# Scheduling a 2387-us hybrid trunk kernel with the detailed machine model instead of the plain one

## The chip, the cores and the metric

The kernel runs on one NeuronCore of a Trainium2 chip. The metric is the device time of one execution in microseconds, taken as the median over runs. Each engine of the core (TensorE for matmuls, VectorE, ScalarE, GpSimd, and SyncE, which here only issues DMAs) works through its own list of instructions in the order in which the compiler left it, and waits at an instruction until the semaphores it needs have been raised by the others. In the rows below PE is TensorE, DVE is VectorE, ACT is ScalarE, SP is SyncE.

## The reference

Input is x of shape (1, 512, 1024) in float32. Each of two layers computes

```
h = RMSNorm(x)
P = h @ W_in            # columns for four mixers and four gates
A: Mamba-2 SSD          # chunked scan, 8 chunks of 64 rows
B: DSA sparse attention # 8 heads, 4 query tiles of 128 rows
C: RWKV-7               # delta-rule state, 8 heads, 8 chunks of 64 rows
D: S5                   # diagonal complex SSM
m = sum_n sigmoid(gate_n(h)) * (y_n @ W_branch_n);  x = x + m @ W_out
x = x + SwiGLU(RMSNorm(x))
```

and a final RMSNorm follows. All of it is float32.

## The kernel before

The large products (projections, gates, branch products, W_out and the feed-forward) are the **bulk**. A weight panel of 128x1024 is loaded into one of two `raw` buffers by a DMA on SP's queue (L286), cast to `wh` on ScalarE (L287), and the remainder `wl` is subtracted on VectorE (L288). For each 128x512 result TensorE then does three matmuls for each of eight slices of the depth: `hh` by `wh` (L294), `hl` by `wh` (L295) and `hh` by `wl` (L296), 24 matmuls in all. What they write is named `pj` (projections and gates), `pb` (branches) or `pf` (feed-forward).

The **mixers** are chains of small steps.

- `dsa()` (L601-666) has 32 steps: 8 heads, each with four query tiles of 128 rows against 128, 256, 384 and 512 keys. A step is a product `lgp` (L645), a bias add (L647), a masked maximum (L648), its negation (L651), an exponential on ScalarE (L652), a reciprocal (L653), a scaling (L654), transposes `ptp` (L657), a copy (L659) and the product with the values, `po` (L661).
- `rwkv_half()` (L1085-1304) runs twice, for heads 0-3 (half 0) and 4-7 (half 1). It forms the blocks of a triangular system (`rwA` L1157, masked on VectorE L1159, scaled L1161), sends them to DRAM (L1168) and back into another layout `NZ` (L1173), copies (L1175) and inverts them in 30 steps of two VectorE instructions (L1180, L1182), sends the inverse to DRAM (L1183, L1185) and back (L1188, L1190), completes it with small products (`zx` L1195, `zz` L1200), and then scans the eight chunks one after another: `bkt` (L1212, L1216), `rwP` (L1233, L1236), a copy on ScalarE (L1240), `rwU` (L1243), an add on VectorE (L1245), `rwS` (L1252), the state's update on VectorE (L1257, L1259), and the output `rwP` (L1264). Each chunk needs the state of the last.
- `ssd()` (L1308-1460) and `s5()` (around L883-1015) are similar; S5 loads its input with eight DMAs per half (L971, `s5UX`).

`Trunk.layer(i)` traces all this in program order:

```python
        with self.at("m", "Tb"):
            self.s5("B")
        with self.at("m", "Ta"):
            y[1] = self.dsa("A")
        self.fill(FILL[0])
        ...
            self.rwkv_half(0, y[2], "B")
        self.fill(FILL[1])
        with self.at("m", "Ta"):
            self.rwkv_half(1, y[2], "A")
        self.fill(FILL[2])
        with self.at("m", "Tb"):
            y[0] = self.ssd("B")
```

`fill(n)` traces n gate panels of bulk, and `FILL = (22, 4, 6)` (L63) says how many stand after which mixer. `at(kind)` gives what is traced a priority: weight loads come before mixers, mixers before bulk. The tile context then plays the program on a model of the machine: at each point it appends to an engine's list that instruction which the model holds to be ready and whose priority is first. So the priorities and the model's durations together fix the order of each list, and on the chip that order is kept. PSUM has two buffers for bulk results and three for each of the two mixer tags, and half 1 of RWKV uses the working slots that DSA frees.

The whole is one launch:

## Time and profile before

| | before |
| --- | --- |
| three runs | 2386.46, 2387.46, 2395.36 us; median 2387.46 us |
| profiled execution, span from first to last instruction | 2387.2 us |
| TensorE busy | 2337.6 us, 98% |
| VectorE busy | 1448.5 us, 61% |
| ScalarE busy | 909.7 us, 38% |
| GpSimd busy | 103.5 us, 4% |
| mean granted TensorE clock | 0.988 of full speed |

The profiled execution's span lies 0.3 us under the median of the runs, so what lies around the span is left out of account, and a sum can be made against 2387.2 us. A matmul's shown time overlaps that of the next; the interval from start to start says what one costs TensorE when it doesn't wait.

### The profile page before, as it was taken

How to read it: one execution, taken by the hardware profiler on the slowest of the kernel's cores; microseconds unless marked ns; L12 is line 12 of the kernel's file. 1: busy time of each engine (PE TensorE's matmuls, PEld its weight loads, DVE VectorE, ACT ScalarE, POOL GpSimd, SP SyncE). 2: the span in 40 equal slices, each digit the busy share in tenths (PEclk: the TensorE clock that was granted, in tenths of full speed). 3: DMA queues.
4: the chain of work that ended last, by engine and by line, in shares of the span. 5: the costliest groups of instructions: out<-in, count | busy, mean ns of one | idle time of the engine just before them, and what ended most of it. 6: DMA issues, size and time to landing. Idle time of an engine off the chain costs nothing.

```text
span 2387.2 us, 32092 instructions
## 1 busy us (share of the span) xinstructions
PE 2337.6 (98%) x12348; PEld 1858.2 (78%) x12348; DVE 1448.5 (61%) x2744; ACT 909.7 (38%) x1459; POOL 103.5 (4%) x180
## 2 busy tenths in 40 slices
PE   7999999999999999999999999999999999999998
PEld 5887767777778888887878787677777788888786
DVE  6569656767578687543343693578667775444333
ACT  6342454434452343322232334543345433222222
POOL 3210000000000101000021000000000000000000
PEclk9999999999999999999998999999999999999999
DMA  7545442334157435433375454324242663333332
GB/s 213 131 114 153 120 157 80 100 94 133 41 175 228 117 100 161 127 97 102 114 198 129 119 158 132 118 83 110 67 142 65 205 194 91 97 97 97 92 97 84
DMA packets 421680, 294.18 MB, mean 123 GB/s; under 512 B 56624, under 2 KB 378240, under 8 KB 419928
## 3 DMA queue, kind: packets, MB, share of 16 engines
q1 hardware_dynamic: 412016, 265.58, 38.0%
q0 software_dynamic: 8512, 26.43, 4.1%
q8 instruction: 97, 1.59, 0.3%
q14 instruction: 55, 0.45, 0.1%
q10 hardware_dynamic: 1000, 0.13, 0.0%
HBM read 237.27 MB, written 51.40 MB: 121 GB/s over the span
## 4 chain that ended last, share of the span: by engine, by line
PE 89%; DVE 5%; DMA 1%; issue 1%; ACT 1%; SPq 0%; POOL 0%; DVEq 0%; ACTq 0%; POOLq 0%
PE pj L295 18%; PE pj L294 18%; PE pj L296 18%; PE pf L296 3%; PE pf L294 3%; PE pf L295 3%; PE pb L294 3%; PE pb L296 2%; PE pb L295 2%; PE lgp L645 2%; PE po L661 2%; DVE wl L288 1%; PE rwA L1157 1%; PE ptp L657 1%; PE rwP L1236 1%
## 5 line engine op out<-in xcount | busy, mean ns | idle before, releaser
L294 PE MATMUL pj<-hh,wh 128*128 128x512 f32 x1888 | 750.0, 398 | 2.8 <-ACT hh L274 1.5
L296 PE MATMUL pj<-hh,wl 128*128 128x512 f32 x1888 | 746.9, 396 | 1.0 <-DVE wl L288 1.0
L295 PE MATMUL pj<-hl,wh 128*128 128x512 f32 x1888 | 747.9, 396 | 0.0
L287 ACT CAST wh<-raw 128x1024 fp32r<-128x1024 f32 x336 | 348.8, 1038 | 947.2 <-PE pj L295 370.6
L288 DVE TENSOR_TENSOR wl<-raw,wh 128x1024 fp32r<-128x1024 f32 x336 | 405.0, 1205 | 388.4 <-ACT wh L287 379.4
L294 PEld LDWEIGHTS pj<-hh,wh 128*128 128x128 f32 x1888 | 355.5, 188 | 85.3 <-issue 7.6
L296 PEld LDWEIGHTS pj<-hh,wl 128*128 128x128 f32 x1888 | 355.1, 188 | 81.0 <-issue 5.8
L295 PEld LDWEIGHTS pj<-hl,wh 128*128 128x128 f32 x1888 | 355.3, 188 | 80.6 <-issue 6.9
L294 PE MATMUL pf<-hid,wh 128*128 128x512 f32 x352 | 137.9, 392 | 1.6 <-ACT wh L287 1.6
L296 PE MATMUL pf<-hid,wl 128*128 128x512 f32 x352 | 137.7, 392 | 0.5 <-DVE wl L288 0.5
L295 PE MATMUL pf<-hid,wh 128*128 128x512 f32 x352 | 137.0, 390 | 0.0
L294 PE MATMUL pb<-yh,wh 128*128 128x512 f32 x256 | 101.8, 398 | 0.0
L295 PE MATMUL pb<-yl,wh 128*128 128x512 f32 x256 | 100.7, 393 | 0.0
L296 PE MATMUL pb<-yh,wl 128*128 128x512 f32 x256 | 100.4, 392 | 0.0
L528 DVE TENSOR_TENSOR fa<-fa,pj 128x512 f32<-128x512 f32 x44 | 30.2, 686 | 95.4 <-PE pj L296 95.3
L525 DVE TENSOR_TENSOR fa<-pj,rb 128x512 f32<-128x512 f32 x44 | 30.4, 690 | 88.7 <-PE pj L296 88.7
L294 PEld LDWEIGHTS pf<-hid,wh 128*128 128x128 f32 x352 | 66.1, 188 | 16.8 <-ACT wh L287 3.4
L296 PEld LDWEIGHTS pf<-hid,wl 128*128 128x128 f32 x352 | 66.1, 188 | 16.0 <-DVE wl L288 2.6
L295 PEld LDWEIGHTS pf<-hid,wh 128*128 128x128 f32 x352 | 66.1, 188 | 13.5
L652 ACT ACTIVATE lg<-lg,nm 128x128 f32<-128x128 f32 (+1 forms) x64 | 35.9, 561 | 78.0 <-DVE nm L651 77.8
L294 PEld LDWEIGHTS pb<-yh,wh 128*128 128x128 f32 x256 | 48.1, 188 | 11.5 <-issue 0.8
L661 PEld LDWEIGHTS po<-p_t,qkvo 128*64 128x64 f32 x320 | 33.2, 136 | 29.8 <-ACT p_t L659 21.1
(482 smaller groups left out, 3144.5 us busy)
## 6 DMA issues: line engine op xcount, KB each, us to landing
raw<-in_w_in SPq DMA_DIRECT2D x146, 512.0 KB
raw<-in_ffn_w SPq DMA_DIRECT2D x120, 512.0 KB
gates<-gate SPq DMA_DIRECT2D x64, 256.0 KB
gld<-gates SPq DMA_DIRECT2D x64, 256.0 KB
raw<-in_w_branch SPq DMA_DIRECT2D x32, 512.0 KB
raw<-in_w_out SPq DMA_DIRECT2D x16, 512.0 KB
raw<-in_ffn_w SPq DMA_DIRECT2D x16, 384.0 KB
s5xs<-s5UX SPq DMA_DIRECT2D x16, 256.0 KB
```

Of the source, the lines that this page charges most:

```text
L287: nc.scalar.copy(wh[:, :n], raw[:, :n])
L288: nc.vector.tensor_sub(wl[:, :n], raw[:, :n], wh[:, :n].bitcast(F32))
L294: mm(ps, wh, ah, start=first, stop=False)
L295: mm(ps, wh, al, start=False, stop=False)
L296: mm(ps, wl, ah, start=False, stop=last)
L525: nc.vector.tensor_mul(a, p1, rb)
L528: nc.vector.tensor_mul(a, a, p3)
L645: mm(ps[:, :W], q[rows, qt * 128:(qt + 1) * 128], k[rows, :W], start=True, stop=True)
L652: nc.scalar.activation(t[:, :W], t[:, :W], AF.Exp, bias=nm, accum_out=sm[:, qt:qt + 1])
L657: nc.tensor.transpose(pt[:, b * 128:(b + 1) * 128], t[:, b * 128:(b + 1) * 128], self.ident)
L661: mm(po[rows, qt * 128:(qt + 1) * 128], vt[:, b, rows], p_t[:, b * 128:(b + 1) * 128], start=(b == 0), stop=(b == qt))
L1157: mm(pa[:, (c - c0) * 128:(c - c0 + 1) * 128], BK[rows, hp, c], AR[rows, hp, c], start=True, stop=True)
```

## The change

```diff
-    with tile.TileContext(nc) as tc:
+    with tile.TileContext(nc, schedule_with_timeline_sim=True) as tc:
         trunk(tc, ins, out)
```

The program, its buffers, priorities, shapes and counts stay. TensorE, VectorE, GpSimd and SP have the same instructions as before; ScalarE has 15 fewer loads of its function tables (37 where 52 were). What the change moves is the order on each engine, since the model that decides what is ready is another one. Bulk and mixer work alternate on TensorE 333 times before and 175 times now. Three places show it.

On TensorE, a chunk of the scan of RWKV half 0 in layer 0 (`rwP`, `rwU`, `rwS` with the matrix M; `pj` is bulk; `lgp`, `ptp`, `po` belong to attention). Before, from the fourth chunk:

```order
L1236 MATMUL rwP<-UV,M_3260 64x64 x2
L294 MATMUL pj<-hh,wh 128x512
L295 MATMUL pj<-hl,wh 128x512
L296 MATMUL pj<-hh,wl 128x512
L294 MATMUL pj<-hh,wh 128x512
L1243 MATMUL rwU<-rwPe,M_3259 64x64 x2
L1243 MATMUL rwU<-rwPe,M_3260 64x64 x2
L295 MATMUL pj<-hl,wh 128x512
L296 MATMUL pj<-hh,wl 128x512
L294 MATMUL pj<-hh,wh 128x512
L295 MATMUL pj<-hl,wh 128x512
L1252 MATMUL rwS<-UV,bkts 128x128 x2
```

And the same place of the fourth chunk in the changed kernel:

```order
L1236 MATMUL rwP<-UV,M_3260 64x64 x2
L657 MATMUL ptp<-cst,lg 128x128 x2
L645 MATMUL lgp<-qkvo 128x384
L1243 MATMUL rwU<-rwPe,M_3259 64x64 x2
L1243 MATMUL rwU<-rwPe,M_3260 64x64 x2
L661 MATMUL po<-p_t,qkvo 64x128 x2
L1252 MATMUL rwS<-UV,bkts 128x128 x2
L1264 MATMUL rwP<-UV,M_3259 64x64 x2
```

The bulk has gone from between the steps of the chunk and a step of attention stands there. Over the eight chunks of half 0 there stood 72 bulk matmuls (59 in layer 1) and now stands none; three heads of attention, which before had ended by then, take part of the room. The bulk that stood here went to earlier places: the early steps of attention now have 18 to 100 bulk matmuls between them. Between the last `rwA` of half 0 and its first `zx` stood 228 bulk matmuls in layer 0 and 207 in layer 1; now 87 and 85 stand there, with some 34 instructions of attention. For half 1 the numbers at that place are 190 and 203 before, and 231 in both layers now. In the scan of half 1, 57 and 55 bulk matmuls stood between first and last chunk; now 38 stand there, all near its first and last chunk, and the six chunks in the middle share TensorE with 111 small matmuls of SSD alone.

On VectorE, the start of the inversion of half 0 in layer 0 (L1175 copies what the load L1173 brought; L647 to L654 belong to attention). Before:

```order
L647 TENSOR_TENSOR lg<-lgp,bias 128x256
L648 ISA lg,mx<-lg,mask 128x256
L648 ISA mx 128x1
L1175 COPY NZ<-NZ 64x1024
L651 TENSOR_SCALAR nm<-mx 128x1
L1180 TENSOR_TENSOR rwv<-NZ 64x30
L1182 TENSOR_TENSOR NZ<-NZ,rwv 64x30
```

And in the changed kernel:

```order
L1159 TENSOR_TENSOR M_3260<-rwA,cst 128x512 x2
L1161 TENSOR_TENSOR M_3260<-M_3260,rwrn 64x16x64
L288 TENSOR_TENSOR wl<-raw,wh 128x1024
L1175 COPY NZ<-NZ 64x1024
L1180 TENSOR_TENSOR rwv<-NZ 64x30
L1182 TENSOR_TENSOR NZ<-NZ,rwv 64x30
L1180 TENSOR_TENSOR rwv<-NZ 64x58
L1182 TENSOR_TENSOR NZ<-NZ,rwv 64x29x2
```

The copy that waits for the way through DRAM and back now stands one instruction behind L1161, whose result is sent on that way; before, 18 rows of attention and `wl` stood between the two. In layer 0 half 1 and layer 1 half 1 it is also one instruction now (10 and 11 rows before), in layer 1 half 0 six (16 before).

On SP's queue, the loads of S5's input in layer 1. Before:

```order
L949 DMA ud<-us 128x512
L971 DMA s5UX<-ud 16x16x64
L286 DMA raw<-in_w_in 128x8x128
L971 DMA s5UX<-ud 16x16x64 x2
L286 DMA raw<-in_w_in 128x8x128
L971 DMA s5UX<-ud 16x16x64
L286 DMA raw<-in_w_in 128x8x128
L971 DMA s5UX<-ud 16x16x64
L286 DMA raw<-in_w_in 128x8x128
```

And in the changed kernel:

```order
L286 DMA raw<-in_w_in 128x8x128
L971 DMA s5UX<-ud 16x16x64 x6
L286 DMA raw<-in_w_in 128x8x128
L949 DMA ud<-us 128x512
L971 DMA s5UX<-ud 16x16x64 x2
L949 DMA ud<-us 128x512
L286 DMA raw<-in_w_in 128x8x128
L987 DMA s5xs<-s5UX 64x1024
```

The eight loads stood between weight loads, each of which waits for a free `raw` buffer; now they stand nearly together.

## Rows read from the trace of the kernel before

**Rows 1.** The page: engines' busy time, and the chain that ended last

```profile
PE 2337.6 (98%) x12348; PEld 1858.2 (78%) x12348; DVE 1448.5 (61%) x2744; ACT 909.7 (38%) x1459; POOL 103.5 (4%) x180
...
PE 89%; DVE 5%; DMA 1%; issue 1%; ACT 1%; SPq 0%; POOL 0%; DVEq 0%; ACTq 0%; POOLq 0%
```

**Rows 2.** Stretches: length, each engine's busy time, granted clock, DMA share, GB/s

```profile
720.00:780.00 60.00, 60.00 (x267) 49.68 (x266) 49.39 (x69) 16.93 (x21) 0.00 (x0) 1.00 0.69 222
...
1293.80:1310.80 17.00, 17.00 (x69) 15.94 (x69) 1.75 (x2) 1.17 (x2) 4.99 (x7) 0.50 0.39 118
1205.00:1211.80 6.80, 5.26 (x16) 3.77 (x16) 5.11 (x9) 2.41 (x4) 0.06 (x1) 0.50 0.64 224
```

**Rows 3.** What PE waited for: us in all, times, longest

```profile
PE xtp L213 <- DMA cst<-in_cst: 14.3, 1, 14.3
PE ptp L657 <- DVE lg L654: 4.7, 7, 1.2
PE s5py L1012 <- DVE s5xs L1005: 4.2, 3, 2.6
PE nrms L249 <- DVE acc L241: 2.9, 1, 2.9
...
PE zx L1195 <- DMA zts<-zt: 0.3, 1, 0.3
```

**Rows 4.** Timeline, DVE, inversion's start in half 0: start, duration, instruction

```profile
422.40 1.22 DVE L1161 TENSOR_TENSOR M<-M,rwrn 64x1024 f32<-64x1024 f32 x1
...
438.64 0.68 DVE L1175 COPY NZ<-NZ 64x1024 f32<-64x1024 f32 x1
```

**Rows 5.** Timeline of SP's queue, the load that this start waits for

```profile
433.35 0.46 SPq L1173 DMA_DIRECT2D NZ<-zd  x1
```

**Rows 6.** DVE's groups in the stretch of that inversion, 439 to 484

```profile
L1180 DVE TENSOR_TENSOR rwv<-NZ 64x30 f32<-64x30 f32 (+14 forms) x30 | 9.6, 321 | 0.5
L1182 DVE TENSOR_TENSOR NZ<-NZ,rwv 64x30 f32<-64x30 f32 (+14 forms) x30 | 9.5, 317 | 0.4
L288 DVE TENSOR_TENSOR wl<-raw,wh 128x1024 fp32r<-128x1024 f32 x6 | 7.3, 1215 | 0.9 <-ACT wh L287 0.9
```

**Rows 7.** Timeline of DVE, SP's queue and PE: the inversion's end to zx

```profile
483.38 0.17 DVE L1182 TENSOR_TENSOR NZ<-NZ,rwv 64x30 f32<-64x30 f32 x1
...
491.35 0.46 SPq L1188 DMA_DIRECT2D zts<-zt  x1
...
495.96 1.19 PE L1195 MATMUL zx<-zts,M 32*32 32x32 f32 x32
```

**Rows 8.** PE's groups between the last rwA and zx, 424 to 496

```profile
L294 PE MATMUL pj<-hh,wh 128*128 128x512 f32 x73 | 29.0, 398 | 0.0
```

**Rows 9.** Timeline of one chunk of the scan, half 0, layer 0

```profile
518.79 0.28 PE L1243 MATMUL rwU<-rwPe,M 64*64 64x64 f32 x2
...
519.10 0.42 DVE L1245 TENSOR_TENSOR UV<-rwU,rwrn 64x256 f32<-64x256 f32 x1 [3.26 <-PE rwU L1243]
...
523.99 0.26 ACT L1240 COPY rwPe<-rwP 64x128 f32<-64x128 f32 x1 [0.52 <-PE rwP L1236]
...
524.30 0.67 PE L1243 MATMUL rwU<-rwPe,M 64*64 64x64 f32 x8
```

**Rows 10.** PE's groups in that scan, 511 to 556

```profile
L296 PE MATMUL pj<-hh,wl 128*128 128x512 f32 x25 | 11.1, 442 | 0.0
```

**Rows 11.** Timeline of one step of attention at 512 keys, layer 0

```profile
396.22 1.12 PE L645 MATMUL lgp<-qkvo 64*128 64x512 f32 x2
...
397.27 0.87 PE L661 MATMUL po<-p_t,qkvo 128*64 128x128 f32 x6
...
398.07 0.50 PE L295 MATMUL pj<-hl,wh 128*128 128x512 f32 x1
...
401.40 0.60 PE L657 MATMUL ptp<-cst,lg 128*128 128x128 f32 x4
...
401.93 0.48 PE L645 MATMUL lgp<-qkvo 64*128 64x128 f32 x2
```

## The prediction

> **What bounds the kernel now.** I read the page first. TensorE is busy 98% of the span and carries 89% of the chain that ended last [rows 1]. The list of its waits confirms that: after the 14.3 us for the constants at the start there are fifteen further entries, from 4.7 us down to 0.3 [rows 3], 26 us together. Then the stretches: in one that holds only bulk, 267 matmuls take 60.00 us, so a bulk matmul costs 0.2247 us, and the clock is at its full level [rows 2]. So the time before is TensorE's own work. A new order can win little, since those 26 us are all that could be saved; it can lose whatever waits it brings. The question is where TensorE's list no longer holds enough independent work to cover the mixers' chains. I went through the new order with the durations of the old trace.
>
> **The change part by part.** The same places occur in both layers, so I price one layer and double it. Bulk moved out of a stretch costs the same where it goes; what counts is the cover that is missing.
>
> *Inversion of half 0.* Before, between the last product `rwA` and the first `zx`, 72 us pass, with 73 bulk matmuls of each of the three lines (219 recorded) beside attention [rows 8]. In the new order 87 (85) bulk matmuls stand there and 33 (36) instructions of attention: 87 × 0.2247 = 19.5 us and some 9.5 us, together 29 us of cover. Attention's 9.5 us come from its step at 512 keys: the products take 1.05 us (396.22 to 397.27), `po` 0.80 (397.27 to 398.07), the transposes 0.53 (401.40 to 401.93) [rows 11]; that is 2.4 us, about 1.5 for the mean over the four widths, and five to six steps stand there.
> The chain to be covered is: the product L1161, 1.2 us; the way through DRAM, from 423.62 (422.40 + 1.22) to the copy at 438.64, 15.0 us [rows 4]; the inversion's 60 instructions, 9.6 + 9.5 = 19.1 us [rows 6]; the way back, from 483.55 to `zx` at 495.96, 12.4 us [rows 7]. The two ways include time in queues. Their lower bounds: the load alone took 438.64 − 433.35 = 5.3 us [rows 4, 5], on the way back 495.96 − 491.35 = 4.6 us [rows 7]; a store and a load as long give 10.6 and 9.2. I take 13 and 12, between them. VectorE now stops at the copy while the DMA runs, because the copy stands directly behind L1161 and the engine works in order. So the `wl` subtractions for the 87 matmuls (four at 1.2 us, [rows 6]) and the VectorE part of attention (five steps of some 1.5 us) come behind the copy, into the inversion: I take 28 us for it, with 19 and 31 as bounds. Sum 1.2 + 13 + 28 + 12 = 54 us against 29: **25 us** of waiting (bounds 11 and 30). Before, the same chain cost nothing because 219 bulk matmuls lay over it.
>
> *Scan of half 0.* Here no bulk stands any more. A chunk's chain took 5.5 us from `rwU` (518.79) to the next `rwU` (524.30) [rows 9], some bulk included. In the stretch of the scan 25 matmuls of each bulk line (about 74) take 16.6 us of 45 [rows 10], so TensorE's own part is 28 us for seven and a half chunks, 3.7 us each. Three heads of attention, twelve steps of 1.5 us, now lie in the scan: 18 us. With `zx`, `zz` and the output's products the stretch holds about 57 us of TensorE work. The chain is 7 us for `zx` and `zz` (four rounds of 1.2 us and the copies between), eight chunks, and about 8 us of normalisation at the end, where before 32 bulk matmuls lay. A step of attention has its own chain from `lgp` to `ptp`, 396.22 to 401.40, 5.2 us [rows 11], which uses VectorE and ScalarE too, and both chains wait for each other on each in-order list. I take 7 us a chunk instead of 5.5: 7 + 56 + 8 = 71, less 57: **14 us** (bounds 0, if a chunk stays at 5.5, and 26, at 8.5).
>
> *Inversion of half 1.* Now 231 bulk matmuls, 52 us, against 1.2 + 13 + 19 + 12 us and ten `wl` in between (12 us): 57. The `wl` that stand behind the copy are late as well while VectorE waits 13 us, and the panels that TensorE has ready run out. **8 us** (0 to 15).
>
> *Scan of half 1.* The six middle chunks have 111 small SSD matmuls beside them and no bulk. TensorE's work there is about 31 us, 5.2 per chunk; at 7 us per chunk **11 us** are missing (0 to 20, the latter since SSD's own chain uses VectorE and ScalarE).
>
> Warm, that is 25 + 14 + 8 + 11 = 58 us a layer (11 to 91).
>
> *The clock.* [...] If all of the scan of half 0 ran at 0.50, a chunk with its attention would need 2 × (3.7 + 1.7) = 10.8 us instead of 7, 30 us over eight chunks, and with the ends 38; the six chunks of half 1 2 × 5.2 = 10.4 instead of 7, 20, with the ends 25. That is 63 us a layer at most and 0 at least; I take half, **32 us**.
> [...]
>
> *S5 at the start of layer 1.* Its input loads stand together on SP now, so S5 can begin sooner, and the 17.0 us stretch at half clock behind its wait may vanish: **−8 us** (0 to −15, with the waits for `s5xs` and the norm, 4.2 and 2.9 us, partly saved [rows 3]). The 15 ScalarE table loads that vanish lie under TensorE's work; without that cover, inside the chains, they would give back a microsecond or two of the waits above. I count them at nothing.
>
> Sum: 2 × (58 + 32) − 8 = 172 us. On 2387.2 us that is **2559, rounded 2560 us**; the median of the runs is 0.3 us higher than the span, which changes nothing.
>
> **The rivals.**
> *The clock stays low through both scans.* Then 63 instead of 32 a layer: 2387 + 2 × 121 − 8 = 2621 us. [...] With every bound at its worst, 2 × (91 + 63) gives 2695.
> *Only the waits count.* The clock recovers between them: 2387 + 116 − 8 = 2495; with the waits at half their size 2440.
> *The cover suffices.* If the round trips go at their bounds, and attention's steps and the chunks dovetail as the model that ordered them assumes, nothing is lost: 2387 ± 12 us, the change doesn't move the time. For it: the scheduler chose these places as ready. Against it: 54 us of chain over 29 us of work needs all the bounds at once.
> *Faster.* If besides that the S5 start saves its waits and its low clock, 7 to 15 us: 2372 to 2380. The point where it decides is where what both scans and inversions lose is under 4 us a layer.
>
> **How the numbers follow.** The forecast (2525 to 2600) has a chance of 0.38, the low clock throughout (2600 to 2695) 0.22, the waits alone (2430 to 2525) 0.27, no change 0.05, faster 0.03, and 0.05 lies beyond or between. A measurement of this kernel tells about 0.5% (12 us) from no change. The range 2440 to 2690 leaves out the two cases at the near side and what lies beyond; chances: faster 0.03, same 0.05, slower 0.92.
>
> **What would show it.** TensorE's waits: in place of the few microseconds of now, some 20 us or more for `zx` or for attention's `lg` behind the copy L1175, in each layer; waits of `rwU` for `rwPe`, of `ptp` for `lg` and of `rwS` for UV that sum to over 20 us a layer; `pj` waiting for `wl` in half 1's inversion. Granted clock well under 0.9 in the scans' stretches, at full in the bulk. A shorter start of layer 1. The prediction is wrong if the scans' stretches last about as long as their work, if the way through DRAM is far under 10 us, or if a place that I priced at nothing (SSD's chain, the branch products, the feed-forward) shows large waits.

## The result and the profile after

The changed kernel takes **2492.04 us** (median of four runs, 2485.41 to 2497.62); the kernel before 2391.41 us on the same chips (2386.46 to 2396.30). The ratio is 1.0418, 95% interval 1.0393 to 1.0444: 100 us slower. Forecast were 172 us, 2560 us, with a range of 2440 to 2690.

The page of the changed kernel, engines' busy time:

```profile
span 2486.6 us, 32063 instructions
...
PE 2389.0 (96%) x12348; PEld 1907.7 (77%) x12348; DVE 1456.8 (59%) x2744; ACT 890.3 (36%) x1444; POOL 103.7 (4%) x180
```

Beside [rows 1]: the span is 99.4 us longer. TensorE's busy time rose by 2389.0 − 2337.6 = 51.4 us with the same 12348 matmuls, and its idle time by (2486.6 − 2389.0) − (2387.2 − 2337.6) = 48.0 us. The matmuls are the same; that they take longer goes with the granted clock (0.953 in the mean, 0.988 before).

What TensorE waited for, us in all, times, longest:

```profile
PE ptp L657 <- DVE lg L654: 18.9, 8, 4.2
...
PE pb L295 <- DVE yl L314: 5.5, 2, 2.8
PE rwS L1252 <- DVE UV L1245: 4.7, 10, 0.5
PE sdns L249 <- DVE sdsq L1454: 4.3, 2, 2.2
PE zx L1195 <- DMA zts<-zt: 4.3, 2, 2.9
...
PE rwU L1243 <- ACT rwPe L1240: 3.3, 9, 0.7
...
PE sdst L1403 <- ACT sdex L1389: 2.8, 2, 1.4
...
PE pb L294 <- DVE m L468: 2.2, 2, 1.2
```

The seven waits of `ptp` before made 4.7 us [rows 3]; now there are eight with 18.9, and the scan's waits (`rwS`, `rwU`) are new, and so are those of SSD (`sdns`, `sdst`) and of the branch products (`pb`). The wait for `s5py`, 4.2 us before, has shrunk to 0.4.

Where it happens, in stretches of the changed kernel (length, then busy time of PE, PEld, DVE, ACT, POOL, granted clock, DMA share, GB/s). The first four cut up the first bulk-free stretch of layer 0 at the first `zx`, the first `rwU` and the last `rwU`; the fifth is the second bulk-free stretch, the last two are those of layer 1:

```profile
432.10:456.10 24.00, 12.58 (x38) 6.91 (x37) 17.06 (x58) 5.10 (x12) 0.54 (x1) 0.55 0.29 65
456.10:477.10 21.00, 20.96 (x170) 14.32 (x170) 4.93 (x16) 7.41 (x19) 0.54 (x1) 0.50 0.12 29
477.10:522.30 45.20, 41.91 (x317) 31.06 (x317) 23.86 (x86) 17.06 (x56) 0.54 (x1) 0.94 0.11 32
522.30:539.10 16.80, 13.50 (x57) 7.57 (x55) 11.67 (x30) 8.41 (x16) 0.31 (x1) 0.80 0.09 30
676.80:746.60 69.80, 63.22 (x606) 51.03 (x605) 38.64 (x94) 28.31 (x71) 0.00 (x0) 0.71 0.17 58
1654.50:1767.70 113.20, 96.87 (x577) 65.61 (x576) 57.86 (x188) 38.64 (x105) 2.69 (x4) 0.67 0.15 40
1905.50:1972.60 67.10, 59.97 (x607) 48.03 (x605) 39.25 (x95) 28.34 (x71) 0.00 (x0) 0.77 0.18 60
```

The four stretches take 107.0, 69.8, 113.2 and 67.1 us, 357 in all. The idle time in them is 18.1 + 6.6 + 16.3 + 7.1 = 48.1 us, as much as the whole increase. Elsewhere TensorE waits as long in all as it did in the whole kernel before (49.5 and 49.6 us), though not for the same things: the waits of the branch products, 7.7 us, come right behind the second stretch of each layer and are new, and most of S5's waits are gone. The norm at the start of layer 1 begins at 1261.33 us, where it began at 1203.11: layer 0 lost 58.2 us, layer 1 the other 41.2.

The start of the inversion of half 0, which the prediction put at 54 us for the whole chain (VectorE's and SP's timelines, then the first `zx`):

```profile
410.61 1.22 DVE L1161 TENSOR_TENSOR M<-M,rwrn 64x1024 f32<-64x1024 f32 x1
415.48 1.23 DVE L288 TENSOR_TENSOR wl<-raw,wh 128x1024 fp32r<-128x1024 f32 x1 [3.65 <-ACT wh L287]
417.88 0.69 DVE L1175 COPY NZ<-NZ 64x1024 f32<-64x1024 f32 x1 [1.18 <-DMA NZ<-zd]
...
411.86 0.85 SPq L1168 DMA_DIRECT2D zd<-M  x2
414.19 0.46 SPq L1173 DMA_DIRECT2D NZ<-zd  x1
...
449.66 0.18 DVE L1182 TENSOR_TENSOR NZ<-NZ,rwv 64x30 f32<-64x30 f32 x1
...
456.13 1.06 PE L1195 MATMUL zx<-zts,M 32*32 32x32 f32 x16 [2.91 <-DMA zts<-zt]
```

The way through DRAM took 417.88 − 411.83 = 6.0 us, where 15.0 stood before [rows 4], and the way back 456.13 − 449.84 = 6.3, where it was 12.4 [rows 7]. On SP's queue the store now goes out at once and the load 2.3 us later; before, the load was issued 9.7 us after the product [rows 4, 5], with loads of weights and gates ahead of it. VectorE waited 1.18 us for the load; its longer pause, 3.65 us, was for the cast `wh` that the `wl` between the product and the copy needs.

### The profile page after: what moved, and what is told of

Its sections match the earlier page's. It is cut to its first block, busy times and chain, and to the rows that moved or that the text cites. A ratio compares the mean times of both kernels' runs of the same rounds, so it can differ in the third digit from the quotient of the medians.

```text
span 2486.6 us, 32063 instructions
## 1 busy us (share of the span) xinstructions
PE 2389.0 (96%) x12348; PEld 1907.7 (77%) x12348; DVE 1456.8 (59%) x2744; ACT 890.3 (36%) x1444; POOL 103.7 (4%) x180
## 5 line engine op out<-in xcount | busy, mean ns | idle before, releaser
L294 PEld LDWEIGHTS pf<-hid,wh 128*128 128x128 f32 x352 | 66.1, 188 | 13.8
L296 PEld LDWEIGHTS pf<-hid,wl 128*128 128x128 f32 x352 | 66.1, 188 | 13.6
L295 PEld LDWEIGHTS pf<-hid,wh 128*128 128x128 f32 x352 | 66.1, 188 | 13.6
L647 DVE TENSOR_TENSOR lg<-lgp,bias 128x128 f32<-128x128 f32 (+1 forms) x64 | 31.1, 486 | 74.5 <-PE lgp L645 74.1
L645 PE MATMUL lgp<-qkvo 64*128 64x128 f32 (+3 forms) x128 | 62.7, 576 | 0.0
```

The costliest lines, as they stand in the source:

```text
L294: mm(ps, wh, ah, start=first, stop=False)
L295: mm(ps, wh, al, start=False, stop=False)
L296: mm(ps, wl, ah, start=False, stop=last)
L645: mm(ps[:, :W], q[rows, qt * 128:(qt + 1) * 128], k[rows, :W], start=True, stop=True)
L647: nc.vector.tensor_add(t[:, :W], ps[:, :W], bias[:, 384 - 128 * qt:512])
```

## The experiments

All but one fix the order themselves. After the program is traced, each engine's instructions are tied to a list, so that the scheduler has no choice left:

```diff
     with tile.TileContext(nc) as tc:
         trunk(tc, ins, out)
+        pin(nc, tc)
```

```python
for prev, i in zip(engine_list, engine_list[1:]):
    tc.add_manual_dep(i, prev.name, DependencyInfo(NoSync, DATA), reason="pin")
```

The list is the plain order, the changed order, or pieces of both: the first piece is taken up to a point in its own order (given in us of TensorE work from the start), the next goes on with what is left. A list by itself moves little where it is the plain one: in trial 11, plain through layer 0, the norm of layer 1 begins at 1203.09 us (1203.11 before). The kernels whose list begins with the changed order (trials 1, 2, 6, 8 and 9) wait 3.3 to 4.9 us for `wl` near 157 us, which the changed kernel doesn't; why isn't shown, and it weighs on each of them.

**1. Both starts changed, the middle plain.** `list = changed[:300] + plain[:1157] + changed[:1400] + plain`

> Same instructions; each engine's order is taken in pieces: the changed order up to 300 us of TensorE work (head 1 of attention, layer 0), the plain order to the end of layer 0, the changed order for the start of layer 1 up to its first attention head, the plain order for the rest. So both layers' four bulk-free stretches are gone and the changed starts of the layers stay. Theory (the loss lies in those stretches alone, and the rest of the changed order is quicker): 2362 to 2374 us, 0.6 to 1.0% under the kernel before. Rival (the changed order gains nowhere): 2385 to 2400 us.

Measured: 2407.85 us, ratio to before 1.0073 (1.0047 to 1.0099). Neither expectation: the bulk-free stretches were gone and the kernel still lost some 17 us. The profile puts most of it at the cuts, which stand inside attention: at the first one four steps ran bare with some 8 us of waits, at the second one `ptp` waited 9.7 us. The trial says that these two cuts inside attention cost about what the kernel lost, and little more.

**2. Changed up to the first bulk-free stretch of layer 0, then plain.** `list = changed[:410.9] + plain`

> The changed order up to the last bulk matmul ahead of the first bulk-free stretch in layer 0 (410.9 us of TensorE work), the plain order for all that is left, layer 1 included. Theory A (the bulk that could cover has been spent early between attention's steps): the loss of layer 0 stays, 35 us or more, 2422 us or more. Theory B (the stretch is bulk-free because attention's last heads are spread over the scan, and the projections of half 1 wait for the buffers that attention frees): the plain order ends attention first, the projections of half 1 then cover the scan, and layer 0 loses under 25 us: 2395 to 2412 us.

Measured: 2445.14 us, ratio 1.0232 (1.0207 to 1.0256), 55 us, theory A. The plain order does finish attention first and then covers the scan with the projections of half 1, as theory B has it, but now attention's last heads are bare. The stretch of this kernel:

```profile
435.40:519.10 83.70, 55.76 (x154) 29.24 (x153) 30.66 (x101) 19.66 (x51) 1.61 (x3) 0.53 0.07 21
```

83.7 us for 154 matmuls, at a granted clock of 0.53. So the plain order, going on from there, doesn't win the loss back: the bulk that it would put beside these heads has been spent. That no other order could is not shown.

**3. Where the bulk was spent.** That is read from the changed kernel's own trace. One step of attention's early heads, VectorE's scaling and the transposes that need it, and the next step's:

```profile
302.19 0.42 DVE L654 TENSOR_SCALAR lg<-lg,rs 128x384 f32<-128x384 f32 x1
...
307.78 0.49 PE L657 MATMUL ptp<-cst,lg 128*128 128x128 f32 x3
...
312.77 0.49 DVE L654 TENSOR_SCALAR lg<-lg,rs 128x512 f32<-128x512 f32 x1
...
316.77 0.38 PE L657 MATMUL ptp<-cst,lg 128*128 128x128 f32 x2
```

The scaled logits were ready at 302.61 and 313.26, and TensorE came for them 5.2 and 3.5 us later, since bulk stood in front. Added up in this way over the 16 steps of heads 0 to 3, finished steps lie waiting 67.5 us in layer 0 and 67.8 in layer 1; in the kernel before 10.4 and 6.4. Some 57 us of bulk in layer 0 and 61 in layer 1 cover a chain that was already over. This is a reading of the trace; no trial moved these steps alone.

**4. Gates moved behind the scans**, the one trial with the scheduler of the change.

```diff
-FILL = (22, 4, 6)
+FILL = (0, 22, 10)
```

> The changed kernel with the gate panels moved: none behind attention, 22 behind half 0 of RWKV, 10 behind half 1, where 22, 4 and 6 stood. The bulk-free stretches get shorter, 46 and 36 us of TensorE work in layer 0 and 54 and 36 in layer 1, where 64 and 45 stood in each. Theory (the loss goes with the bulk-free work): about 139 us times 172/218, that is some 29 us less, 2455 to 2475. Rival (gates aren't what covers there, attention's spread sets the loss): 2485 to 2500.

Measured: 2526.91 us, ratio to before 1.0547 (1.0517 to 1.0578), by the ratios some 31 us slower than the change. The theory that the loss goes with the amount of bulk-free work is wrong in this form. The detailed model again put the gates between early steps (of the scan, whose first three chunks took some 20 us each) and left attention's last steps bare. The first stretch of layer 0 is shorter, 96.4 us in place of 107.0, but TensorE is idle for 25.9 us of it where it was idle for 18.1; where the rest of the 31 us arose was not followed up.

```profile
PE ptp L657 <- DVE lg L654: 46.0, 22, 3.3
```

```profile
441.70:538.10 96.40, 70.50 (x316) 41.61 (x314) 43.35 (x142) 29.91 (x80) 1.92 (x4) 0.68 0.12 36
```

**5. Attention in the plain order, all that follows in layer 0 in the changed one.** `list = plain[:432] + changed[:1157] + plain`

> The plain order to the end of attention in layer 0 (432 us of TensorE work), the changed order from there to the end of layer 0, the plain order for layer 1. The scan of half 0 is then bulk-free (36 us of work), but no attention is left in it; the second stretch is as in the changed kernel. Theory (attention left over from its stretched early steps makes most of the first stretch's loss): the scan adds 10 to 20 us to the second stretch's 18 to 28, 2420 to 2440. Rival (a scan without bulk costs the whole by itself): 2455 or more.

Measured: 2466.89 us, ratio 1.0318 (1.0289 to 1.0347), 75 us for layer 0 alone: the rival. The waits and the first bulk-free stretch of this kernel (up to the first `zx`, to the first `rwU`, the scan, the end):

```profile
PE zx L1195 <- DMA zts<-zt: 19.0, 1, 19.0
```

```profile
466.20:485.30 19.10, 0.12 (x1) 0.00 (x0) 11.83 (x32) 1.01 (x1) 0.00 (x0) 0.61 0.31 69
485.30:498.00 12.70, 11.35 (x147) 9.44 (x147) 0.00 (x0) 3.93 (x9) 0.00 (x0) 0.50 0.17 44
498.00:546.90 48.90, 42.08 (x256) 33.17 (x256) 15.86 (x47) 10.90 (x36) 0.00 (x0) 0.57 0.02 6
546.90:563.20 16.30, 10.65 (x32) 5.37 (x30) 8.24 (x18) 4.49 (x9) 0.31 (x1) 0.50 0.09 30
```

Without attention in it the stretch still takes 97.0 us. RWKV's chain alone takes them at a granted clock of 0.50 to 0.61: the end of the inversion, 19 us with nothing on TensorE, the small products, a scan of 48.9 us, and 16.3 us of normalisation. At this clock attention's leftover steps aren't what makes the stretch long; they fill part of it, and beside them the clock in layer 0's scan was 0.94 instead of 0.57. How long it would be without them at full clock isn't shown. Each of the two chains took 84 to 97 us when it was bare, at 0.53 (trial 2) and 0.50 to 0.61 (trial 5), both at once 107.

**6, 7. Each stretch of layer 0 alone.** `list = changed[:475] + plain` and `list = plain[:550] + changed[:1157] + plain`

> The changed order up to the end of the first bulk-free stretch in layer 0 (475 us of TensorE work), the plain order for all the rest: the first stretch alone. If the stretches' losses add up: 40 to 50 us above the kernel before, 2430 to 2445. If the changed order takes most of it back behind the stretch: under 30 us.

> The plain order up to 550 us of TensorE work in layer 0 (behind the scan of half 0), the changed order to the end of layer 0, the plain order for layer 1: the second bulk-free stretch alone (scan of half 1 and SSD). If the stretches' losses add up: 18 to 28 us above the kernel before, 2410 to 2422. If only attention's part counts: under 8 us.

Measured: 2438.16 us, ratio 1.0193 (1.0166 to 1.0221), 46 us; and 2420.83 us, ratio 1.0111 (1.0080 to 1.0143), 27 us. Together 73 us, where layer 0 of the change lost 58. In the first trial 4.4 us of the surplus is the wait for `wl` at 157 us. In the second the cut moved the `zx` of half 1, which came 33.8 us after its inversion (8.1 in the change); whether that cost time isn't shown, and most of the 15 us stays open.

**8. Pauses filled with work.** Extra 128x512 matmuls stand ahead of attention's transposes (and of `zx`), where TensorE waits in the first stretch:

```diff
-                    pt = self.P("ptp")
+                    pt = self.P("ptp"); warm(self, pt, h, qt)
```

```python
for _ in range(WARM.get((h, qt), 0)):
    nc.tensor.matmul(pt, hh[:, 0, :128], hh[:, 0], start=True, stop=True)
```

> The changed order, and in each layer 4 times 12 extra 128x512 matmuls of 0.225 us directly ahead of the transposes of head 4 (tiles 1 to 3) and head 5 (tile 0), where TensorE waited 1.9 to 4.2 us; the transposes overwrite what they write. 96 matmuls, 21.6 us more work. If the half clock of the first stretch is what follows those waits and costs time: the clock stays up into the scan and the time falls by 10 to 25 us, to 2465 to 2482. If the chains set the time there whatever the clock: no gain, 2490 to 2505.

> The changed order with extra 128x512 matmuls, whose results are overwritten, in the first bulk-free stretch of both layers: 12 ahead of three steps of attention's head 4, 16 ahead of the first zx, 4 and 3 times 6 in head 5, 4 times 6 in head 6; 98 in each layer, 22 us of work. In the run with fewer of them the clock fell again at zx in layer 0 (122 us for the stretch) and stayed up in layer 1 (106 us). Theory (the half clock costs about a third of its length): if the clock now stays up in both layers, both stretches take 95 to 106 us. If the clock is up and a stretch still takes 110 us or more, the chains set the time and the clock costs little there.

> The changed order with fewer extra matmuls in the first stretch of both layers: 10 ahead of three steps of head 4, 14 ahead of the first zx, 2 ahead of each later step up to head 6: 58 in each layer, 13 us, 9 us less than in the kernel with 98. Their results are overwritten. If those 98 kept the clock up but delayed the chains by what they cost: the clock stays up and the stretches take 98 us or less, where 107.8 and 106.8 stood. If the chains set the length: 104 us or more with the clock up.

Measured: 2502.11 us (ratio to before 1.0459, 1.0433 to 1.0486), 2488.29 us (1.0385, 1.0345 to 1.0424) and 2481.90 us (1.0395, 1.0359 to 1.0430), beside the change's 1.0418. The last two are no slower than the change although TensorE does 44 and 26 us more. The first stretches of layers 0 and 1, in the kernel with 98 extra matmuls a layer and in that with 58:

```profile
437.50:545.30 107.80, 98.81 (x675) 69.14 (x674) 57.33 (x189) 37.85 (x102) 1.92 (x4) 0.94 0.15 38
1660.70:1767.50 106.80, 97.05 (x676) 68.23 (x675) 57.58 (x188) 38.43 (x105) 1.92 (x4) 0.95 0.15 42
```

```profile
434.70:540.90 106.20, 95.28 (x635) 65.54 (x634) 57.38 (x189) 38.06 (x102) 1.92 (x4) 0.87 0.16 39
1650.60:1749.50 98.90, 87.77 (x635) 60.73 (x634) 57.47 (x188) 38.30 (x105) 1.92 (x4) 0.95 0.16 46
```

With the pauses filled the clock is higher: 0.94 and 0.95 with 98, 0.87 and 0.95 with 58, in place of 0.74 (the mean over the four parts above) and 0.67. The stretches get hardly shorter with 98, and with 58 one takes 106.2 us and the other falls from 113.2 to 98.9. That lies between the two theories. Layer 1's stretch, cut up as before, tells them apart: up to the first `zx`, to the first `rwU`, and the scan, in the changed kernel, in that with 58 and in that with 98:

```profile
1654.50:1678.30 23.80, 11.94 (x31) 5.83 (x30) 16.60 (x55) 5.27 (x13) 1.31 (x1) 0.55 0.30 71
1678.30:1696.70 18.40, 18.39 (x167) 13.68 (x167) 3.26 (x12) 6.49 (x18) 0.00 (x0) 0.50 0.13 29
1696.70:1750.40 53.70, 50.88 (x325) 36.92 (x325) 26.57 (x92) 18.59 (x60) 1.07 (x2) 0.79 0.09 28
```

```profile
1650.60:1674.40 23.80, 19.08 (x76) 12.50 (x75) 16.42 (x55) 5.27 (x13) 0.54 (x1) 0.93 0.36 90
1674.40:1685.60 11.20, 11.20 (x171) 8.56 (x170) 3.04 (x11) 5.80 (x16) 0.00 (x0) 1.00 0.04 13
1685.60:1733.00 47.40, 44.27 (x339) 32.25 (x339) 26.55 (x95) 19.03 (x60) 1.07 (x2) 1.00 0.11 32
```

```profile
1660.70:1685.10 24.40, 20.61 (x84) 14.26 (x83) 16.50 (x55) 5.25 (x13) 0.54 (x1) 0.93 0.35 84
1685.10:1698.20 13.10, 13.10 (x179) 10.00 (x178) 3.04 (x11) 5.90 (x16) 0.00 (x0) 1.00 0.04 11
1698.20:1751.20 53.00, 49.88 (x363) 36.77 (x363) 26.57 (x95) 19.04 (x60) 1.07 (x2) 1.00 0.09 28
```

Ahead of `zx` the chain sets the length: 23.8, 23.8 and 24.4 us, with 31, 76 and 84 matmuls and the clock at 0.55, 0.93 and 0.93. Behind it TensorE does. Up to the first `rwU` it is busy without a pause in all three kernels, and the 32 matmuls that the last kernel has more than the one before it in the last two parts (8 and 24, 7.2 us of work) make them 7.5 us longer at full clock, 66.1 us instead of 58.6. So there an extra matmul costs what it takes, and the lower clock (0.50 and 0.79) costs time as well: 72.1 us became 58.6, and without the extra matmuls it would be some 55.5 (an estimate: the 14 that stand there, at 0.2247 us each). The extra work hid what the clock gave back. In layer 0 the scan ran at 0.94 without it, and there was less to win. Each of these figures is from one profiled execution.

**9. More alternations.** In the changed order 63 bulk matmuls beside the S5 blocks are put one by one between the S5 products.

> The changed order, but 63 bulk matmuls beside the four blocks of S5 products stand one by one between the small products instead of ahead of or behind them. If each change between bulk and small matmuls costs TensorE time (0.33 us for a bulk matmul behind a small one and 0.28 us for one ahead of it, instead of 0.23): 0.2 us each, 12 to 15 us more, about 2505, and as much more busy time. Rival (the bulk ran closer in the changed kernel for another reason): within 4 us of the changed kernel.

Measured: 2510.52 us, ratio to before 1.0513 (1.0479 to 1.0546), slower than the change, as the theory had it, but not for its reason. A piece of the alternation:

```profile
116.18 0.33 PE L1012 MATMUL s5py<-s5xs,s5O 128*128 128x64 f32 x2
116.31 0.48 PE L294 MATMUL pj<-hh,wh 128*128 128x512 f32 x1
116.64 0.33 PE L1011 MATMUL s5py<-s5UX,s5T 128*128 128x64 f32 x2
116.77 0.48 PE L295 MATMUL pj<-hl,wh 128*128 128x512 f32 x1
```

And its wait for the states of S5:

```profile
PE s5py L1012 <- DVE s5xs L1005: 10.2, 3, 3.5
```

A small product and a bulk matmul together take 116.64 − 116.18 = 0.46 us. In blocks a small product takes 0.22 and a bulk matmul 0.22 us, 0.45 together. The bulk matmul behind a small one starts its successor later, 0.33 us, but the small one before it took 0.13. So alternating costs 0.01 us, nothing; what the profile shows instead are 10.2 us of waits for `s5xs` (0.4 in the change), and further waits for `wl`; they may come from the bulk that stood ahead of the small products and now stands between them. Busy time rose by 1.8 us alone (2390.8, 2389.0 in the change). The theory falls.

**10, 11. Only the start of layer 1 changed.** `list = plain[:1157] + changed[:1300] + plain`, and the same with 1255

> The plain order for layer 0, the changed order for the start of layer 1 (norm and both halves of S5, up to 1300 us of TensorE work, ahead of attention's first step), the plain order for the rest. In the first spliced kernel the start of layer 1 was some 9 to 13 us quicker, but the cuts inside attention cost 23. Theory (the earlier S5 loads are a real gain): 8 to 13 us under the kernel before, a ratio of 0.9945 to 0.9965. Rival (the gain was a shift that the rest takes back, or the cut costs as much): within 4 us of before.

> As the kernel before it, but with the cut behind the first half of S5 (1255 us of TensorE work). Theory: 5 to 10 us under the kernel before, since the second half's wait of 1.0 us and its 10 us at half clock come back; less than the cut at 1300 gains. Rival: within 4 us of before.

Measured: 2386.88 us, ratio 0.9966 (0.9946 to 0.9986), and **2379.75 us, ratio 0.9933 (0.9906 to 0.9959)**. The second beats both kernels, by more than expected; that the earlier cut gains more was not expected. In its profile, the wait of `s5py`, and the stretch from 1260 to 1320 us:

```profile
PE s5py L1012 <- DVE s5xs L1005: 1.6, 2, 1.0
```

```profile
1260.00:1320.00 60.00, 60.00 (x303) 50.71 (x302) 18.25 (x24) 18.20 (x25) 6.78 (x10) 1.00 0.49 129
```

The wait of 2.6 us and the stretch of 17.0 us at a clock of 0.50 behind it [rows 2, 3] are gone. In the kernel before, the wait ended at 1293.24 and the stretch began at 1293.80:

```profile
1293.24 0.43 PE L1012 MATMUL s5py<-s5xs,s5O 128*128 128x64 f32 x2 [2.56 <-DVE s5xs L1005]
```

With the cut at 1300 attention then starts without enough in hand, and `ptp` waits 3.1 us at one place.

## Why the prediction was right, and where its sums were off

*What bounds the kernel, and where it would lose.* Right in the main: nearly all of the loss lies in the two bulk-free stretches of each layer, as waits of `ptp`, `rwS`, `rwU` and `zx` and as a lower granted clock (0.67 to 0.77 in the stretches). But two of the prediction's own signs of being wrong showed as well. The way through DRAM was well under 10 us, and two places priced at nothing have waits: SSD's chain in the second stretches (`sdns` and `sdst`, 7.1 us, half of TensorE's idle time there) and the branch products behind them (`pb`, 7.7 us). The sign was nearly sure for this reason: 98% busy leaves a new order little to gain.

*The number.* Of the forecast 172 us 100 came, and that they lie in a range 250 us wide shows little. The time falls into the band of the rival without a low clock (2430 to 2525), whose account isn't what happened: 51.4 us of the increase are longer busy time. The term that was too large is the waits, 58 us a layer; TensorE's idle time in the stretches is 24.6 us in layer 0 and 23.5 in layer 1.

*Inversion of half 0, 25 us.* It measured 11.4 us in layer 0 (waits of 4.2, 2.3, 2.0 and 2.9) and 11.5 in layer 1. The mis-sized terms are the two ways through DRAM: 13 and 12 us assumed, 5.8 to 6.2 and 6.3 to 8.2 measured in the four halves, below the lower bounds of 10.6 and 9.2. I took the old ways as mostly transfer and bounded a store by a load as long as the one shown. But of the 15.0 us there 9.7 passed before SP's queue issued the load; the change moved that order too, and I had gone through TensorE's and VectorE's lists there and not through SP's. Nor was 5.3 us the load's: VectorE didn't wait for it in the old trace but came to the copy late by its own list. In the change, where it does wait, 3.5 to 3.8 us pass from the issue to the copy. The inversion itself was 32.0 us with what lies in it, just over the bound of 31.

*The copy that stops VectorE.* It doesn't stand directly behind the product, as the prediction has it, but behind one `wl` or more, and VectorE waited 1.2 us for it (0.8 to 2.5 in the other three halves), where 13 were assumed.

*Scan of half 0, 14 us.* In layer 0 chunks took 6.5 us in the mean, (522.3 − 477.1) / 7, at a clock of 0.94; 7 was assumed. In layer 1, at 0.79, the scan took 53.7 us instead of 45.2. The ends were longer: 21.0 us from `zx` to the first `rwU` instead of 7, at a clock of 0.50, with attention's steps in between and TensorE busy for 20.96 of them, and 16.8 us of normalisation instead of 8. TensorE's waits in these three parts come to 6.6 us, not 14. The stretch alone cost 46 us (trial 6), where the inversion, the scan and half of the clock's price made 25 + 14 + 19 = 58.

*Inversion of half 1, 8 us.* The sum there, 57 against 52, gave 5, and 8 was taken. It was nothing: from the last `rwA` to `zx` 53.1 us pass, and TensorE's waits for `wl` come to 1.2 us in the whole run.

*Scan of half 1, 11 us, and its clock, 12.5.* 23.5 forecast; the stretch took 69.8 and 67.1 us for 45 us of work, 23 more in the mean, and 27 by itself (trial 7). The size was right, though half of the waits in it are SSD's.

*The clock, 32 us a layer.* The size was about right. The clock fell to 0.67 to 0.77 in the stretches, though not in layer 0's scan of half 0 (0.94), which is why the rival that priced the low clock throughout at 63 us a layer failed. Of the 58.2 us that layer 0 lost, 24.6 are idle time in its stretches and some 4 the branch products' waits; what is left, some 30 us, is longer busy time (an estimate by subtraction). In layer 1's first stretch the parts behind `zx` show it directly: 13.5 us less at full clock, and by the estimate of trial 8 some 17 without the extra matmuls. Ahead of `zx` the low clock cost nothing, since the chain set the length there: 23.8 us at 0.55 and at 0.93 (trial 8). No run shows both scans wholly at 0.50, from which the 63 us and the 32 as their half were worked out; the lowest clock read in a scan is 0.57 (trial 5). What the trace of the change shows: in the first stretches up to the first `rwU`, with waits of 1.4 to 4.2 us and one of 0.35, the granted clock was 0.55 and then 0.50 in both layers; in the scans of half 0, whose waits are 0.9 us at most, it was 0.94 in layer 0 and 0.79 in layer 1.

*S5 at the start of layer 1, −8 us.* Right in sign, and more: 10 to 22 us by the interval of trial 11.

*What the prediction did not see* is why the cover is missing; it took that as a given of the order. The trace shows some 4 us more bulk than needed in front of each of attention's first 16 steps (trial 3), and that bulk is gone later. That this is the cause is argued from the reading, not tested by a trial of its own, and what the detailed model's numbers have wrong there the runs don't show. Nor did the prediction see that half 0's chain would fill the stretch at a clock of 0.50 to 0.61 even without attention (trial 5).

Summed up per layer: 58 us lost in layer 0, and 41 in layer 1, which is 57 if its start gained the 16 us of trial 11.

## What to carry to other kernels

Where one kind of work covers several chains in turn, look at how long finished steps lie waiting early on, not only at where an engine waits later: cover that is spent on a chain which is already over can be missing at the next one, and moving panels about under the same planner made it worse in the one trial of that here. When an order changes, go through the DMA queue's list as well, and see whether the engine at the end really waited, before the old distance between a store and the load behind it is taken as a transfer's time. And price a low clock part by part: ahead of `zx`, where TensorE waited for the chain, it cost nothing here (23.8 us at 0.55 and at 0.93), and behind `zx`, where TensorE was busy for 69.3 of 72.1 us, 13.5 us (58.6 us at 1.00 with 14 matmuls more).

## What was unexpected of the hardware

A bulk matmul behind a small product takes 0.33 us from start to start, but the small one ahead of it takes 0.13 instead of 0.22, so the pair costs what its parts cost apart. The way of the blocks through DRAM and back took 5.8 to 6.2 us in the four halves of the change, where nothing stands between the last store and the load in the queue. In layer 1, 44 extra matmuls in TensorE's pauses ahead of `zx` raised the granted clock there from 0.55 to 0.93, and the 23.8 us stayed what they were; behind `zx` 32 extra matmuls made 7.2 us of work and 7.5 us of time.
